# Retention in a two-layer mixer kernel: key decays applied to the values, query decays applied behind the states' products, states laid out by head parity

## The chip, the cores and the metric

One core of a Trainium2 chip runs the whole program. The metric is device time in microseconds of one execution. The core has five engines that run side by side, each through its own instructions in order: TensorE (PE; its weight loads, PEld, are shown apart), VectorE (DVE), ScalarE (ACT), GpSimd (POOL) and SyncE (SP), which issues the DMA transfers here.

## The reference, cut to what matters

Two layers, each with an input projection, four token mixers and an output projection over 2048 + 256 tokens. The change lies in one mixer, retention, with 4 heads of 64 in two directions d:

```
q_dec = exp((idx + 1) * log_gamma)        # per head and position in the chunk
k_dec = exp((c - 1 - idx) * log_gamma)
c_dec = exp(c * log_gamma)
s_new = s * c_dec + einsum('bhcd,bhce->bhde', k * k_dec, v)
o     = einsum('bhcd,bhde->bhce', q * q_dec, s) + einsum('bhij,bhje->bhie', att, v)
```

`k_dec` and `q_dec` are one number per token, head and direction. So k_dec may scale the rows of v in place of those of k, and q_dec may scale the rows of the product q s in place of those of q.

## The kernel before, in words

Tokens are worked in 18 tiles of 128 (`NT`), a retention chunk being one tile. Each layer has four passes. **A** normalises, projects and convolves. **B** holds the chunk-wise work: `gdn_tile` for another mixer, many 64x64 products, and `ret_tile` for retention, beside its projection (`dense`) and the state scans. **C** projects and runs sliding-window attention (`swa_tile`), finishes the scans, and forms the mixers' outputs (`ret_out`, `gdn_out`). **D** is the output projection.

In pass B `ret_tile` copies v (L753), rotates q and k, writes `kd`, the keys times both directions' decays (VectorE, L769), and multiplies: per head `kd` (128 tokens by 128 = direction and feature) by v gives the tile's addition to the state, `KV`, stored in DRAM with the directions in partitions 0 to 63 and 64 to 127. Then `qd`, the queries times both decays (GpSimd, L783), four transposes of q and k (L787), four of `qd` (L793), copies of both by ScalarE (L789, L795), and the store of the transposed `qd` as `Qr` (L796). The local attention follows. `ret_scan` carries the state over the tiles and stores it as `Sr`. In pass C `ret_out` loads `Qr`, `Sr` and the local part, makes one product per head, in which the sum over 128 partitions covers both directions, adds (L853), and normalises per head.

Matrix products go through the helper `mm`, so nearly all of them have line 145; their tiles tell them apart. An f32 product is two records in the trace, an f32 transpose one. A product with 128 rows and 128 columns of weights uses TensorE whole (`128*128` in a row); with 64 columns it uses one of two halves side by side (`128*64`), with 64 rows one of two halves above each other (`64*128`), with both one of four quarters (`64*64`). These are called modes below. PSUM banks are handed out by name: `pm` is a pair (`pm0`, `pm1`), each with one buffer, taken in turn by `self.pm()`.

The order of the instructions on each engine is fixed when the program is built: `weave` interleaves the passes' generators, and `Plan` then sorts all instructions by a table of costs and by the length of the work behind them. Any change of the work so draws the whole order anew.

Of the kernel before, what the change touches and what calls it, by code (L numbers as in the profile page):

```python
# [16 lines left out]
NT = 18  # L17
# [3 lines left out]
TC = 1  # L21
LU = 4
OWN = 1
PMAP = dict(x.split(":") for x in "ptk:0 ptv:h1 pt:0 pu:1 ptq:1 pm0:0 pm1:1 pc0:h0 pc1:h1 po:1 p3:1 rkv:h0 rpt:0 rpt2:0 rpo:h0 ch:h0".split())
PMAP.update(x.split(":") for x in ''.split())
CV = 4
NB = 9
# [6 lines left out]
MULT, ADD, SUB, MAXO, MINO = ALU.mult, ALU.add, ALU.subtract, ALU.max, ALU.min  # L34
# [33 lines left out]
           ("rqkT", 512, 2), ("ratt", 512, 1), ("rD", 512, 1), ("rlo", 256, 1)],  # L68
          [("gA00", 256, 1), ("gQ1", 512, 1), ("gR1", 1024, 1), ("gW1", 1024, 1), ("gMC1", 1024, 1)]),
    "C": ([("sqk", 384, 1), ("sks", 384, 1), ("srope", 256, 2), ("rota", 256, 1), ("rotb", 256, 1), ("sVc", 128, 2), ("sV", 128, 5),  # L70
           ("sqs", 512, 1), ("szt", 512, 1), ("szl", 512, 1), ("shs", 512, 1), ("roq", 512, 1), ("goq", 512, 1), ("goS", 512, 1),
           ("roS", 256, 1), ("roo", 256, 1), ("roz", 256, 1), ("rosq", 256, 1), ("goo", 256, 1), ("gosq", 256, 1), ("goz", 256, 1),
           ("roy", 256, 1), ("goy", 256, 1), ("sy", 256, 2), ("sPT", 640, 2), ("szb", 512, 2), ("sP", 640, 2)],
          [("sqT", 1024, 4)],
# [50 lines left out]
class Net:  # L125
# [134 lines left out]
    def setup(self):  # L260
        nc, cp, dp = self.nc, self.cp, self.dp
        C = self.t(cp, [128, C_W], "C")
        nc.sync.dma_start(C, self.consts[:, :C_W])
        self.C = C
        self.id = C[:, C_ID:C_ID + 128]
        self.bfid = self.t(cp, [128, 128], "bfid", BF)
        nc.vector.tensor_copy(self.bfid, self.id)
        self.bfm = self.t(cp, [128, 256], "bfm", BF)
        ml = self.t(Area([self.U], []), [128, 256], "cml")
        nc.sync.dma_start(ml, self.consts[:, T_ML:T_ML + 256])  # L270
        nc.vector.tensor_copy(self.bfm, ml)
# [12 lines left out]
        self.hT = self.t(dp, [NB, 128, 2 * KT * 256], "hTd")
        self.x1 = self.t(dp, [NTOK, D], "x1")
        self.modd = self.t(dp, [DEPTH, 2, 3 * D], "modd")
        self.gcd = self.t(dp, [NT, 8, 128], "gcd")
        self.hg = self.t(dp, [NB, 128, 6, 256], "hgd")
        self.gz = self.t(dp, [NT, 128, 256], "gzd")
        self.rz = self.t(dp, [NT, 128, 256], "rzd")  # L290
        self.MC = self.t(dp, [36, 128, 512], "MCd")
        self.Sg = self.t(dp, [36, 128, 256], "Sgd")
        self.Qg = self.t(dp, [NT, 128, 512], "Qgd")
        self.Qr = self.t(dp, [NT, 128, 512], "Qrd")
        self.KV = self.t(dp, [NT, 128, 256], "KVd")
        self.Sr = self.t(dp, [NT, 128, 256], "Srd")
        self.Og = self.t(dp, [NT, 128, 256], "Ogd")
        self.Or = self.t(dp, [NT, 128, 256], "Ord")
        self.law = self.t(dp, [NB, 128, 2, 2, 256], "lawd")
        self.hl = self.t(dp, [NB, 128, 2, 256], "hld")  # L300
        self.hb = self.t(dp, [NB, 128, 2, 256], "hbd")
        self.yT = self.t(dp, [NB, 128, 8, 256], "yTd")
# [405 lines left out]
    def ret_setup(self, sp):  # L708
        nc, C = self.nc, self.C
        sm = Area([self.ab.rearrange('p t u -> p (t u)')], [])  # L710
        lg = self.t(sm, [128, 8], "rlg")
        x = self.t(sm, [128, 8], "rlx")
# [13 lines left out]
        io = C[:, C_IOTA:C_IOTA + 4]  # L726
        self.qdec = self.t(sm, [128, 4, 2], "rqd")
        self.kdec = self.t(sm, [128, 4, 2], "rkd")
        self.cdec = self.t(self.lp, [128, 4], "rcd")
        for d in range(2):  # L730
            nc.vector.tensor_scalar(self.qdec[:, :, d], lg[:, 4 * d:4 * d + 4], io[:, 2 * d:2 * d + 1], None, op0=MULT)
            nc.vector.tensor_scalar(self.kdec[:, :, d], lg[:, 4 * d:4 * d + 4], io[:, 2 * d + 1:2 * d + 2], None, op0=MULT)
            nc.vector.tensor_scalar(self.cdec[64 * d:64 * d + 64], lg[64 * d:64 * d + 64, 4 * d:4 * d + 4], 128.0, None, op0=MULT)
        for a in (self.qdec, self.kdec, self.cdec):
            nc.scalar.activation(a, a, AF.Exp)

# [10 lines left out]
    def ret_tile(self, t, pa, pb, pp):  # L747

        nc = self.nc
        q_on = t >= 2 or not self.last  # L750
        qk = self.t(pp, [128, 512], "rqk", bufs=2)
        v = self.t(pp, [128, 256], "rv", bufs=2)
# [10 lines left out]
        else:  # L763
# [1 line left out]
            nc.sync.dma_start(rp, self.rope[(t - 2) * 128:(t - 1) * 128, 0:256])  # L765
            self.rotate(qk[:, :256], pa[:, :256], 4, rp[:, 0:64], rp[:, 64:128], pp)
            self.rotate(qk[:, 256:], pa[:, 256:], 4, rp[:, 128:192], rp[:, 192:256], pp)
        kd = self.t(pp, [128, 4, 2, 64], "rdd")
        nc.vector.tensor_tensor(kd, qk[:, 256:].rearrange("p (h e) -> p h e", h=4)[:, :, None].to_broadcast([128, 4, 2, 64]),  # L769
                                self.kdec[:, :, :, None].to_broadcast([128, 4, 2, 64]), op=MULT)  # L770
        self.taken += 1
        yield 0, 4.02
        pkv = self.slot("rkv", True)
        for h in range(4):
            self.mm(pkv[:, h * 64:(h + 1) * 64], kd[:, h].rearrange("p d e -> p (d e)"), v[:, h * 64:(h + 1) * 64])
        kv = self.t(pp, [128, 256], "rlo")
        nc.scalar.copy(kv, pkv[:, :256])
        self.st('K').dma_start(self.KV[t], kv)
        yield 0.86, 0
        if not q_on:  # L780
            return
        qd = self.t(pp, [128, 4, 2, 64], "rdd")
        nc.gpsimd.tensor_tensor(qd, qk[:, :256].rearrange("p (h e) -> p h e", h=4)[:, :, None].to_broadcast([128, 4, 2, 64]),  # L783
                                self.qdec[:, :, :, None].to_broadcast([128, 4, 2, 64]), op=MULT)
        pt = self.slot("rpt")
        for i in range(4):
            nc.tensor.transpose(pt[:, i * 128:(i + 1) * 128], qk[:, i * 128:(i + 1) * 128], self.id)  # L787
        qkT = self.t(pp, [128, 512], "rqkT", bufs=2)
        nc.scalar.copy(qkT, pt)  # L789
        yield 0.44, 0.84  # L790
        pt2 = self.slot("rpt2")
        for h in range(4):
            nc.tensor.transpose(pt2[:, h * 128:(h + 1) * 128], qd[:, h].rearrange("p d e -> p (d e)"), self.id)  # L793
        qdT = self.t(pp, [128, 512], "rqkT", bufs=2)
        nc.scalar.copy(qdT, pt2)  # L795
        self.st('Q').dma_start(self.Qr[t], qdT)  # L796
        yield 0.44, 2
        pat = self.sc2()
        for hp in range(2):
            for par in range(2):  # L800
# [5 lines left out]
        po = self.slot("rpo", True)  # L806
# [7 lines left out]
    def ret_scan(self, lo, hi):  # L814
        nc = self.nc
        if lo == 0:
            self.rS = self.t(self.lp, [128, 4, 64], "rS", bufs=2)
            nc.vector.memset(self.rS, 0.0)
        fl = lambda a: a.rearrange("p h e -> p (h e)")
        for i in range(lo, hi):  # L820
            S = self.rS
            tf, tb = i, ORDER_B[i]
            yield lambda: tf in self.kvs and tb in self.kvs
            self.st('S').dma_start(self.Sr[tf, 0:64], fl(S)[0:64])
            self.st('S').dma_start(self.Sr[tb, 64:128], fl(S)[64:128])
            self.rstep = i
            if i == NT - 1:
                break
            kv = self.t(self.lp, [128, 4, 64], "rsk", bufs=2)
            nc.sync.dma_start(fl(kv)[0:64], self.KV[tf, 0:64])  # L830
            nc.sync.dma_start(fl(kv)[64:128], self.KV[tb, 64:128])
            S2 = self.t(self.lp, [128, 4, 64], "rS", bufs=2)
            nc.vector.tensor_tensor(S2, S, self.cdec[:, :, None].to_broadcast([128, 4, 64]), op=MULT)
            nc.vector.tensor_tensor(S2, S2, kv, op=ADD)
            self.rS = S2
            yield 0, 1.5

    def ret_out(self, t, pp):

        nc = self.nc  # L840
        s = t % 2
        q = self.t(pp, [128, 512], "roq")
        nc.sync.dma_start(q, self.Qr[t])
        S = self.t(pp, [128, 256], "roS")
        nc.sync.dma_start(S, self.Sr[t])
        o0 = self.t(pp, [128, 256], "roo")
        nc.sync.dma_start(o0, self.Or[t])
        zz = self.t(pp, [128, 256], "roz")
        nc.sync.dma_start(zz, self.rz[t])
        po = self.pm()  # L850
        for h in range(4):
            self.mm(po[:, h * 64:(h + 1) * 64], q[:, h * 128:(h + 1) * 128], S[:, h * 64:(h + 1) * 64])
        nc.vector.tensor_tensor(o0, po[:, :256], o0, op=ADD)  # L853
        o4 = o0.rearrange("p (h e) -> p h e", h=4)
        mu = self.t(pp, [128, 4], "romu")
        nc.vector.tensor_reduce(mu, o4, axis=AX.X, op=ADD)
        nc.vector.tensor_scalar(mu, mu, 1.0 / 64, None, op0=MULT)
# [9 lines left out]
        pt = self.pm()  # L867
# [1173 lines left out]
```

## Time and profile before

| | |
|---|---|
| median of 3 runs | 3140.94 us (3136.82 to 3141.93) |
| the profiled execution | 3140.24 us, its span 3138.5 us |
| PE busy | 2940.4 us, 94% of the span |
| VectorE, ScalarE, GpSimd busy | 62%, 43%, 39% |
| mean granted TensorE clock | 0.969 |

The span runs from the first to the last instruction, and 1.7 us lie around it. PE counts as busy while any matmul is in flight, so 94% says where the time goes, not how well TensorE is filled.

### The profile page before, as it was taken

To read this page: it belongs to the slowest core of one execution; us is meant where nothing else is said; L and a number is where in the kernel's file an instruction comes from. 1 tells how busy PE (TensorE), PEld (TensorE's weight loads), DVE (VectorE), ACT (ScalarE), POOL (GpSimd) and SP (SyncE) were. 2 spreads that over 40 slices of the span, in tenths; PEclk is the share of its full clock that TensorE was granted. 3 is DMA by queue.
4 is the path that set the end of the run, shared out by engine and by line. 5 is a ranking of instruction groups with operands and counts; after the bars stand their busy time and mean duration, and the time that the engine had idled before them with its cause. 6 is when DMAs were issued, how large, how long until landed. Compare 5 with 4: busy or idle time off the path is not lost. (4 is left out here: it accounts for less than half of the span.)

```text
span 3138.5 us, 78206 instructions
## 1 busy us (share of the span) xinstructions
PE 2940.4 (94%) x31820; PEld 2497.3 (80%) x31820; DVE 1938.9 (62%) x4258; ACT 1334.3 (43%) x2930; POOL 1220.2 (39%) x1197
## 2 busy tenths in 40 slices
PE   4999979999999999979999998899999899999987
PEld 3999867778877888867789998678878688888766
DVE  4587777676665576653255787767666456767321
ACT  3466644444443344442134666444444424445211
POOL 2133345555542232334352333456555422323332
PEclk8999989999999999999999999999999999999998
DMA  7243465554456655375652435556444664544431
GB/s 275 95 173 134 166 168 150 167 153 118 134 180 187 199 163 162 122 264 196 197 202 106 162 144 162 161 150 176 141 140 120 220 198 139 171 152 142 153 122 68
DMA packets 410121, 504.69 MB, mean 161 GB/s; under 512 B 94056, under 2 KB 311560, under 8 KB 403104
## 3 DMA queue, kind: packets, MB, share of 16 engines
q1 hardware_dynamic: 409760, 499.68, 49.7%
q8 instruction: 250, 4.10, 0.5%
q14 instruction: 111, 0.91, 0.1%
HBM read 320.06 MB, written 179.50 MB: 159 GB/s over the span
## 5 line engine op out<-in xcount | busy, mean ns | idle before, releaser
L145 PE MATMUL pd<-w,h 128*128 128x512 f32 (+1 forms) x3408 | 984.4, 411 | 26.2 <-DVE U L1560 16.1
L145 PEld LDWEIGHTS pd<-w,h 128*128 128x128 f32 x3408 | 613.4, 192 | 158.6 <-ACT U L1558 18.5
L145 PE MATMUL pd<-h,w 128*128 128x256 f32 x3360 | 589.2, 294 | 1.1 <-DVE U L479 1.1
L145 PEld LDWEIGHTS pd<-h,w 128*128 128x128 f32 x3360 | 479.8, 193 | 10.6 <-issue 5.0
L330 POOL TENSOR_TENSOR U<-U,mh 128x4 f32<-128x4 f32 (+2 forms) x174 | 179.5, 1034 | 379.6 <-DVE U L329 361.2
L145 PE MATMUL pg<-h,w 128*128 128x256 f32 x1680 | 294.3, 294 | 4.7 <-DVE U L1571 3.6
L145 PE MATMUL pm<-U 128*64 128x128 f32 (+4 forms) x3280 | 249.4, 274 | 26.4 <-ACT U L1089 7.7
L145 PEld LDWEIGHTS pg<-h,w 128*128 128x128 f32 x1680 | 245.0, 191 | 9.9 <-DVE U L1571 3.8
L145 PEld LDWEIGHTS pm<-U 128*64 128x64 f32 (+2 forms) x3280 | 197.6, 143 | 68.4 <-issue 22.3
L145 PE MATMUL pg<-w,h 128*128 128x512 f32 x816 | 228.6, 394 | 1.3 <-DVE U L1571 1.3
L145 PEld LDWEIGHTS <-U 64*64 64x64 f16 x6512 | 153.2, 109 | 55.1 <-issue 45.4
L145 PE MATMUL pg<-U 64*64 64x64 f16 x6512 | 188.4, 195 | 1.2 <-DVE U L1031 1.1
L145 PEld LDWEIGHTS pg<-w,h 128*128 128x128 f32 x816 | 154.4, 190 | 38.8 <-issue 3.3
L1031 DVE TENSOR_TENSOR U<-pg,C 128x512 f16<-128x512 f32 x180 | 122.0, 684 | 64.3 <-PE pg L145 63.5
L625 DVE SCALAR_TENSOR_TENSOR U<-U 128x256 f32<-128x256 f32 x318 | 159.8, 552 | 1.1 <-POOL U L558 1.1
L1560 DVE TENSOR_TENSOR U<-U 128x1 f32<-128x1 f32 x34 | 7.7, 230 | 234.9 <-ACT U L1558 234.9
L1456 ACT ACTIVATE U<-sc,U 128x640 f32<-128x640 f32 (+2 forms) x136 | 104.2, 766 | 103.7 <-DVE U L1454 88.5
L1471 ACT COPY U<-pg 128x512 f32<-128x512 f32 (+2 forms) x248 | 100.7, 436 | 103.6 <-PE pg L1470 50.1
L1558 ACT ACTIVATE U<-pd 128x512 f32<-128x512 f32 x34 | 20.0, 594 | 276.7 <-PE pd L145 164.4
L1453 DVE TENSOR_REDUCE U<-sc 128x1 f32<-128x640 f32 (+2 forms) x136 | 106.2, 781 | 47.3 <-PE sc L145 45.7
L1046 DVE STREAM_TRANSPOSE U<-U 128x512 f16<-128x512 f16 x144 | 100.8, 703 | 45.8 <-ACT U L1042 45.3
L1042 ACT CAST U<-pg 128x512 f16<-128x512 f32 x144 | 84.0, 588 | 82.9 <-PE pg L145 77.9
(297 smaller groups left out, 6038.3 us busy)
## 6 DMA issues: line engine op xcount, KB each, us to landing
hTd<-h SPq DMA_DIRECT2D x18, 2048.0 KB, 6.7
h<-hTd SPq DMA_DIRECT2D x72, 512.0 KB, 5.6
h<-hTd SPq DMA_DIRECT2D x18, 2048.0 KB, 9.8
MCd<-U SPq DMA_DIRECT2D x72, 256.0 KB, 3.3
cMC<-MCd SPq DMA_DIRECT2D x140, 128.0 KB, 3.3
U<-yTd SPq DMA_DIRECT2D x34, 512.0 KB, 4.5
U<-in_w_in_dram SPq DMA_DIRECT2D x58, 256.0 KB, 3.9
hgd<-U SPq DMA_DIRECT2D x53, 256.0 KB, 2.5
```

Source lines behind the costliest of these rows:

```text
L145: self.nc.tensor.matmul(out, lhsT, rhs, start=start, stop=stop)
L330: nc.gpsimd.tensor_tensor(out, out, self.mh[:, :n], op=ALU.pow)
L625: nc.vector.scalar_tensor_tensor(z[:, i], xb[:, f, j:j + 256], cw[:, f, j:j + 1], z[:, i], op0=MULT, op1=ADD)
L1031: nc.vector.tensor_tensor(M, p1, lev(k), op=MULT)
L1042: nc.scalar.copy(Y, p2)
L1046: nc.vector.transpose(fl(YT), fl(Y))
L1453: nc.vector.tensor_reduce(m[:, h:h + 1], pv, axis=AX.X, op=MAXO)
L1456: nc.scalar.activation(p[:, :nk], pv, AF.Exp, bias=m[:, h:h + 1], accum_out=sums[:, h:h + 1])
L1471: nc.scalar.copy(pT[:, a:a + w], pt[:, :w])
L1558: nc.scalar.activation(x1[:, 512 * k:512 * k + 512], po[k], AF.Square, accum_out=ss[:, k:k + 1])
L1560: nc.vector.tensor_tensor(rs, ss[:, 0:1], ss[:, 1:2], op=ADD)
```

## The change

`kd` is gone: `vd`, the values times both directions' decays, takes its place (same engine, same shape), and the product per head is now k (64 columns of weights) by `vd` (128 columns), so heads of even number fill partitions 0 to 63 and those of odd number 64 to 127. `qd`, its four transposes and their copy are gone; the transposed q, unscaled, is stored instead, half as wide. State, scan and their DRAM tensors are laid out to match: direction outside, parity of the head in the partitions; their transfers are as many as before. In `ret_out` each head's product takes 64 rows, and gives the two directions beside each other (128 columns); the heads of one parity go to one `pm` bank, those of the other to the second. Eight operations of VectorE then each scale 64 columns by the query's decay and add them, where one addition of 256 columns stood.

```diff
-        kd = self.t(pp, [128, 4, 2, 64], "rdd")
-        nc.vector.tensor_tensor(kd, qk[:, 256:].rearrange("p (h e) -> p h e", h=4)[:, :, None].to_broadcast([128, 4, 2, 64]),
+        vd = self.t(pp, [128, 4, 2, 64], "rdd")
+        nc.vector.tensor_tensor(vd, v.rearrange("p (h e) -> p h e", h=4)[:, :, None].to_broadcast([128, 4, 2, 64]),
                                 self.kdec[:, :, :, None].to_broadcast([128, 4, 2, 64]), op=MULT)
...
+        pk4 = pkv[:, :256].rearrange("p (d a f) -> p d a f", d=2, a=2)
         for h in range(4):
-            self.mm(pkv[:, h * 64:(h + 1) * 64], kd[:, h].rearrange("p d e -> p (d e)"), v[:, h * 64:(h + 1) * 64])
+            self.mm(pk4[64 * (h % 2):64 * (h % 2) + 64, :, h // 2], qk[:, 256 + h * 64:256 + (h + 1) * 64], vd[:, h])
...
-        qd = self.t(pp, [128, 4, 2, 64], "rdd")
-        nc.gpsimd.tensor_tensor(qd, qk[:, :256].rearrange("p (h e) -> p h e", h=4)[:, :, None].to_broadcast([128, 4, 2, 64]),
-                                self.qdec[:, :, :, None].to_broadcast([128, 4, 2, 64]), op=MULT)
...
-        pt2 = self.slot("rpt2")
-        for h in range(4):
-            nc.tensor.transpose(pt2[:, h * 128:(h + 1) * 128], qd[:, h].rearrange("p d e -> p (d e)"), self.id)
-        qdT = self.t(pp, [128, 512], "rqkT", bufs=2)
-        nc.scalar.copy(qdT, pt2)
-        self.st('Q').dma_start(self.Qr[t], qdT)
-        yield 0.44, 2
+        self.st('Q').dma_start(self.Qr[t], qkT[:, :256])
...
-        po = self.pm()
-        for h in range(4):
-            self.mm(po[:, h * 64:(h + 1) * 64], q[:, h * 128:(h + 1) * 128], S[:, h * 64:(h + 1) * 64])
-        nc.vector.tensor_tensor(o0, po[:, :256], o0, op=ADD)
+        po = [self.pm()[:, :256].rearrange("p (a d f) -> p a d f", a=2, d=2) for _ in range(2)]
+        for a in range(2):
+            for par in range(2):
+                r = slice(64 * par, 64 * par + 64)
+                self.mm(po[par][:, a], q[r, a * 128:(a + 1) * 128], S[r, :, a])
         o4 = o0.rearrange("p (h e) -> p h e", h=4)
+        for d in range(2):
+            for h in range(4):
+                nc.vector.scalar_tensor_tensor(o4[:, h], po[h % 2][:, h // 2, d], self.qdec[:, h, d:d + 1], o4[:, h], op0=MULT, op1=ADD)
```

The order on PE at the first retention tile of pass B in layer 0, before; `sc_3904` holds the KV products, L787 transposes q and k, L793 `qd`, `pd` is dense work:

```order
L145 MATMUL sc_3904<-G_233 128x64 x4
L787 MATMUL pm_184_4079<-C_96,G_233 128x128 x4
L980 MATMUL pm_185_4085<-C_96,U_87 128x128 x4
L145 MATMUL pd_4178<-w_2_88,h_171_3905 128x512 x2
L793 MATMUL pm_186_4097<-C_96,G_233 128x128 x4
L145 MATMUL sc_3904<-U_87 64x64 x16
```

The same place after the change (lines moved up by one to three; the second `sc_3904` row is the local attention):

```order
L145 MATMUL sc_3904<-G_233 64x2x64 x4
L786 MATMUL pm_184_4078<-C_96,G_233 128x128 x4
L977 MATMUL pm_185_4084<-C_96,U_87 128x128 x4
L145 MATMUL sc_3904<-G_233 128x128 x4
L145 MATMUL pd_4171<-w_2_88,h_171_3905 128x512 x3
```

The KV products are still four in a row, now 64 partitions by 2 x 64, and the transposes of L793 have no row any more.

The order on PE at the third `ret_out` of pass C in layer 0, before; `pm_755` holds its products, `pd` is dense work, `pg` and `sc` belong to the attention:

```order
L1470 MATMUL pg_772_14404<-C_96,U_87 128x128 x2
L145 MATMUL pd_14547<-h_741_14156,w_2_88 128x256 x3
L145 MATMUL pm_755_14270<-U_87 128x64 x4
L1407 MATMUL pm_764_14348<-C_96,U_87 128x128 x2
L145 MATMUL pd_14547<-h_741_14156,w_3_89 128x256 x3
```

And after, where `pm_740` and `pm_739` hold the two parities, and eleven other rows lie between their two groups:

```order
L145 MATMUL pd_14453<-h_725_14046,w_6_92 128x256 x2
L145 MATMUL pd_14453<-h_725_14046,w_7_93 128x256 x3
L145 MATMUL pm_740_14161<-U_87 128x128 x2
L145 MATMUL pd_14453<-h_725_14046,w_8_94 128x256
L145 MATMUL sc_14220<-G_13504,F_13503 128x256 x2
```

The second piece, from the same stretch:

```order
L1467 MATMUL pg_751_14259<-C_96,U_87 128x128 x2
L145 MATMUL sc_14270<-G_13504,F_13503 128x256 x2
L145 MATMUL pd_14453<-h_725_14046,w_3_89 128x256 x2
L145 MATMUL pm_739_14160<-U_87 128x128 x2
L145 MATMUL pd_14453<-h_725_14046,w_3_89 128x256
```

What stood as one group of four is now two groups of two, each of one parity, with whole-array work between. Over the 34 `ret_out` of both layers the 64-row products stand in 56 groups, of which 3 alternate the two halves. Counted over all of PE's order, the mode changes between neighbours 1271 times before and 1380 times after: in the stretches of pass B 893 and 900 times, in those from the end of pass B on (passes C, D, and A of the second layer) 368 and 468 times, ahead of the first pass B 8 and 10 times, and twice at the seams.

The order on VectorE at the same `ret_out`, before (L853 is the addition, L1454 and L1398 the attention's):

```order
L1454 TENSOR_SCALAR U_87<-U_87,rb_236 128x1
L853 TENSOR_TENSOR U_87<-pm_755_14270,U_87 128x256
L856 TENSOR_REDUCE U_87<-U_87 128x4
L857 TENSOR_SCALAR U_87<-U_87 128x4
L1398 TENSOR_TENSOR U_87<-U_87 128x2x64
```

And after:

```order
L1451 TENSOR_SCALAR U_87<-U_87,rb_236 128x1
L851 SCALAR_TENSOR_TENSOR U_87<-pm_739_14160,ab_252,U_87 128x64 x4
L851 SCALAR_TENSOR_TENSOR U_87<-pm_740_14161,ab_252,U_87 128x64 x4
L1342 SCALAR_TENSOR_TENSOR U_87<-U_87 128x512
L853 TENSOR_REDUCE U_87<-U_87 128x4
```

Eight operations on the two banks stand where one on a single bank stood (`ab` holds the decays).

## Rows read from the trace of the kernel before

Times are in microseconds from the span's start unless marked otherwise; "x136" is a count, "mean ns" that of one instruction. In the groups by form the columns behind the count are busy us, mean ns of one, and the idle us before them with what ended it.

**Rows 1.** The page: the span, and part 1's row of the engines
```profile
span 3138.5 us, 78206 instructions
PE 2940.4 (94%) x31820; PEld 2497.3 (80%) x31820; DVE 1938.9 (62%) x4258; ACT 1334.3 (43%) x2930; POOL 1220.2 (39%) x1197
```

**Rows 2.** Busy time by stretch: steady passes B and C of both layers
```profile
core 0: us, PE busy (x) PEld busy (x) DVE busy (x) ACT busy (x) POOL busy (x), PEclk, DMA share, GB/s
430.00:960.00 530.00, 521.15 (x9006) 415.37 (x9006) 347.33 (x654) 223.67 (x458) 278.70 (x246) 1.00 0.53 154
1040.00:1360.00 320.00, 314.04 (x2706) 278.52 (x2704) 227.36 (x637) 153.44 (x418) 98.23 (x121) 0.99 0.49 156
2010.00:2460.00 450.00, 449.37 (x8097) 359.03 (x8098) 300.59 (x583) 194.78 (x396) 247.78 (x219) 1.00 0.51 147
2580.00:2880.00 300.00, 291.20 (x2514) 257.92 (x2512) 206.08 (x574) 140.46 (x385) 87.74 (x110) 0.98 0.47 147
```

**Rows 3.** Groups by form, TensorE's matmuls (PE) and weight loads (PEld), line 793
```profile
L793 PE MATMUL pm<-C,G 128*128 128x128 f32 x136 | 22.1, 284 | 0.0
L793 PEld LDWEIGHTS pm<-C,G 128*128 128x128 f32 x136 | 15.8, 142 | 4.0 <-issue 1.7
```

**Rows 4.** Groups by form, weight loads of small f32 matmuls on line 145
```profile
L145 PEld LDWEIGHTS pm<-U 128*64 128x64 f32 x1824 | 94.3, 141 | 35.1 <-issue 9.0 <-ACT U L1471 8.1 <-DVE U L853 5.0
L145 PEld LDWEIGHTS sc<-G 128*128 128x128 f32 x560 | 73.3, 195 | 16.9 <-DVE G L769 10.6 <-DVE F L999 1.6 <-DVE G L804 0.5
L145 PEld LDWEIGHTS pm<-U 128*128 128x128 f32 x304 | 39.5, 193 | 7.4 <-ACT U L1242 5.4 <-DVE U L1230 0.8
L145 PEld LDWEIGHTS sc<-G 64*128 64x128 f32 x272 | 18.5, 186 | 8.2 <-issue 5.7 <-ACT G L795 0.4 <-ACT U L1106 0.4
```

**Rows 5.** Timeline, PE: a tile's KV products (pass B), a ret_out's (pass C)
```profile
509.84 1.00 PE L145 MATMUL sc<-G 128*128 128x64 f32 x8
510.67 0.60 PE L1105 MATMUL pm<-C,U 128*128 128x128 f32 x4
...
1116.75 1.00 PE L145 MATMUL pm<-U 128*128 128x64 f32 x8
1117.58 0.28 PE L1470 MATMUL pg<-C,U 128*128 128x128 f32 x1
```

**Rows 6.** Timeline, PE, pass C: transposes ahead of a mode change, and without
```profile
1109.15 0.38 PE L869 MATMUL pm<-C,U 128*128 128x128 f32 x2
1109.46 0.43 PE L145 MATMUL pm<-U 128*64 128x128 f32 x2
1109.82 0.98 PE L145 MATMUL pd<-h,w 128*128 128x256 f32 x6
...
1113.16 0.38 PE L1199 MATMUL pm<-C,U 128*128 128x128 f32 x2
1113.30 0.95 PE L145 MATMUL pd<-h,w 128*128 128x256 f32 x6
```

**Rows 7.** Timeline, PEld, the same place: idle time ahead of the loads
```profile
1109.46 0.19 PEld L145 LDWEIGHTS pm<-U 128*64 128x64 f32 x2 [0.17 <-issue]
1109.82 0.54 PEld L145 LDWEIGHTS pd<-h,w 128*128 128x128 f32 x4 [0.17 <-issue]
```

**Rows 8.** Groups by form, VectorE: readings of PSUM, and the shortest operation
```profile
L1479 DVE TENSOR_TENSOR U<-pm,U 128x128 f32<-128x128 f32 x68 | 19.4, 286 | 28.1 <-PE pm L145 27.2
L853 DVE TENSOR_TENSOR U<-pm,U 128x256 f32<-128x256 f32 x34 | 14.3, 419 | 18.6 <-DMA U<-Ord 9.3 <-PE pm L145 9.3
L1458 DVE TENSOR_TENSOR U<-U 128x1 f32<-128x1 f32 x136 | 29.3, 215 | 49.7 <-ACT U L1457 43.8 <-ACT U L1456 5.4
```

**Rows 9.** Groups by form, GpSimd and ScalarE: the two operations taken out
```profile
L783 POOL TENSOR_TENSOR G<-G,ab 128x512 f32<-128x512 f32 x34 | 37.9, 1113 | 73.9 <-PE sc L145 72.6 <-DVE U L954 1.0
...
L795 ACT COPY G<-pm 128x512 f32<-128x512 f32 x34 | 20.0, 587 | 34.9 <-PE pm L793 32.5 <-DMA KVd<-G 2.3
```

**Rows 10.** Timeline, PE, end of pass C, layer 0: its longest wait
```profile
1390.80 2.46 PE L145 MATMUL pm<-U 128*64 128x128 f32 x16 [6.51 <-ACT U L1471]
```

More of the change, by code (lines that the diff above doesn't have):

```diff
@@ L23 @@
 OWN = 1
-PMAP = dict(x.split(":") for x in "ptk:0 ptv:h1 pt:0 pu:1 ptq:1 pm0:0 pm1:1 pc0:h0 pc1:h1 po:1 p3:1 rkv:h0 rpt:0 rpt2:0 rpo:h0 ch:h0".split())
+PMAP = dict(x.split(":") for x in "ptk:0 ptv:h1 pt:0 pu:1 ptq:1 pm0:0 pm1:1 pc0:h0 pc1:h1 po:1 p3:1 rkv:h0 rpt:0 rpo:h0 ch:h0".split())
 PMAP.update(x.split(":") for x in ''.split())
@@ L70 @@
     "C": ([("sqk", 384, 1), ("sks", 384, 1), ("srope", 256, 2), ("rota", 256, 1), ("rotb", 256, 1), ("sVc", 128, 2), ("sV", 128, 5),
-           ("sqs", 512, 1), ("szt", 512, 1), ("szl", 512, 1), ("shs", 512, 1), ("roq", 512, 1), ("goq", 512, 1), ("goS", 512, 1),
+           ("sqs", 512, 1), ("szt", 512, 1), ("szl", 512, 1), ("shs", 512, 1), ("roq", 256, 1), ("goq", 512, 1), ("goS", 512, 1),
            ("roS", 256, 1), ("roo", 256, 1), ("roz", 256, 1), ("rosq", 256, 1), ("goo", 256, 1), ("gosq", 256, 1), ("goz", 256, 1),
@@ L293, in setup @@
         self.Qg = self.t(dp, [NT, 128, 512], "Qgd")
-        self.Qr = self.t(dp, [NT, 128, 512], "Qrd")
-        self.KV = self.t(dp, [NT, 128, 256], "KVd")
-        self.Sr = self.t(dp, [NT, 128, 256], "Srd")
+        self.Qr = self.t(dp, [NT, 128, 256], "Qrd")
+        self.KV = self.t(dp, [NT, 2, 128, 128], "KVd")
+        self.Sr = self.t(dp, [NT, 2, 128, 128], "Srd")
         self.Og = self.t(dp, [NT, 128, 256], "Ogd")
@@ L728, in ret_setup @@
         self.kdec = self.t(sm, [128, 4, 2], "rkd")
-        self.cdec = self.t(self.lp, [128, 4], "rcd")
+        self.cdec = self.t(self.lp, [128, 2, 2], "rcd")
         for d in range(2):
@@ L732, in ret_setup @@
             nc.vector.tensor_scalar(self.kdec[:, :, d], lg[:, 4 * d:4 * d + 4], io[:, 2 * d + 1:2 * d + 2], None, op0=MULT)
-            nc.vector.tensor_scalar(self.cdec[64 * d:64 * d + 64], lg[64 * d:64 * d + 64, 4 * d:4 * d + 4], 128.0, None, op0=MULT)
+            r = slice(64 * d, 64 * d + 64)
+            nc.vector.tensor_scalar(self.cdec[r], lg[r].rearrange("p (d a b) -> p d a b", d=2, a=2)[:, :, :, d], 128.0, None, op0=MULT)
         for a in (self.qdec, self.kdec, self.cdec):
@@ L773, in ret_tile @@
         pkv = self.slot("rkv", True)
+        pk4 = pkv[:, :256].rearrange("p (d a f) -> p d a f", d=2, a=2)
         for h in range(4):
-            self.mm(pkv[:, h * 64:(h + 1) * 64], kd[:, h].rearrange("p d e -> p (d e)"), v[:, h * 64:(h + 1) * 64])
+            self.mm(pk4[64 * (h % 2):64 * (h % 2) + 64, :, h // 2], qk[:, 256 + h * 64:256 + (h + 1) * 64], vd[:, h])
         kv = self.t(pp, [128, 256], "rlo")
         nc.scalar.copy(kv, pkv[:, :256])
-        self.st('K').dma_start(self.KV[t], kv)
+        self.st('K').dma_start(self.KV[t].rearrange("d p n -> p d n"), kv.rearrange("p (d n) -> p d n", d=2))
         yield 0.86, 0
@@ L816, in ret_scan @@
         if lo == 0:
-            self.rS = self.t(self.lp, [128, 4, 64], "rS", bufs=2)
+            self.rS = self.t(self.lp, [128, 2, 2, 64], "rS", bufs=2)
             nc.vector.memset(self.rS, 0.0)
-        fl = lambda a: a.rearrange("p h e -> p (h e)")
+        fl = lambda a: a.rearrange("p a e -> p (a e)")
         for i in range(lo, hi):
@@ L823, in ret_scan @@
             yield lambda: tf in self.kvs and tb in self.kvs
-            self.st('S').dma_start(self.Sr[tf, 0:64], fl(S)[0:64])
-            self.st('S').dma_start(self.Sr[tb, 64:128], fl(S)[64:128])
+            self.st('S').dma_start(self.Sr[tf, 0], fl(S[:, 0]))
+            self.st('S').dma_start(self.Sr[tb, 1], fl(S[:, 1]))
             self.rstep = i
@@ L828, in ret_scan @@
                 break
[L829 to L833, printed above, removed]
+            kv = self.t(self.lp, [128, 2, 2, 64], "rsk", bufs=2)
+            nc.sync.dma_start(fl(kv[:, 0]), self.KV[tf, 0])
+            nc.sync.dma_start(fl(kv[:, 1]), self.KV[tb, 1])
+            S2 = self.t(self.lp, [128, 2, 2, 64], "rS", bufs=2)
+            nc.vector.tensor_tensor(S2, S, self.cdec[:, :, :, None].to_broadcast([128, 2, 2, 64]), op=MULT)
             nc.vector.tensor_tensor(S2, S2, kv, op=ADD)
@@ L841, in ret_out @@
         s = t % 2
-        q = self.t(pp, [128, 512], "roq")
+        q = self.t(pp, [128, 256], "roq")
         nc.sync.dma_start(q, self.Qr[t])
-        S = self.t(pp, [128, 256], "roS")
-        nc.sync.dma_start(S, self.Sr[t])
+        S = self.t(pp, [128, 2, 2, 64], "roS")
+        nc.sync.dma_start(S.rearrange("p d a f -> p d (a f)"), self.Sr[t].rearrange("d p n -> p d n"))
         o0 = self.t(pp, [128, 256], "roo")
```

## The prediction

> **What bounds the kernel now.** I read the page first. PE is busy for 94% of the span, no other engine for more than 62% [rows 1]. Since "busy" is a mean over passes, I then cut the span into its steady stretches, two of pass B and two of pass C [rows 2]: PE is in flight for 521 of 530 us and 449 of 450 in B, for 314 of 320 and 291 of 300 in C, while VectorE has 66% and 67% in B, 71% and 69% in C. PE waits long only at the passes' ends, as where one product waits 6.5 us for the attention's copy [rows 10]. So in the stretches where retention works the end moves by what TensorE's stream gains or loses, and other engines' work is covered as long as PE finds other work ahead of it. PEclk is 0.98 to 1.00 there, so no gain is to be had from the clock. The sum is made against the profiled execution, 3140.24 us; the median of the runs is 0.7 us above it. A measurement of this kernel can tell about 0.2%, some 6.3 us, from no change; the line to "faster" is so at 3134.7.
>
> **The transposes taken out.** 136 transposes on L793 go, four for each of 34 tiles. Their weight loads are busy for 15.8 us, 116 ns each, and their matmuls for 22.1, in which part of a neighbour's flight is counted [rows 3]. I take the loads: **-15.8 us**, bounds -12 and -22 (12: some overlap with a neighbour in any case).
>
> **The KV products.** 36 tiles with four products, eight records, each. Now such a group holds PE for 0.83 us from its start to the next start [rows 5]; the loads of this form take 73.3 / 560 = 131 ns a record when all its groups are counted [rows 4]. After the change the weights have 64 columns and the moving operand 128. The nearest row is that of the attention's and the other mixer's output, 94.3 / 1824 = 52 ns a record [rows 4], in which neighbours alternate between the two halves, as the four heads do here. Eight make 0.41 us, 0.42 less: **-15.1 us** for 36. Bounds: -5 (the pace of 64*128, 18.5 / 272 = 68 ns, and no alternation) and -17.
>
> **The products of ret_out.** 34 tiles, eight records each, 0.83 us [rows 5]. With 64 rows and alternating halves a record is 68 ns [rows 4], which would save 0.29 us a tile. But in the order only 3 of the 56 groups alternate; the others load the same half again and again, for which the nearest row is a whole-array load of 39.5 / 304 = 130 ns [rows 4], about what it costs now. I take 3 of 34 tiles: **-0.9 us**; bounds -9.9 and 0. The Trainium skill ("TensorEngine Tiling (Array Packing)", "Theoretical Speedup") gives up to twofold for a contract dimension of at most 64. By it these products would save 14.1 us; no run here shows it for groups that stay on one half.
>
> **The mode changes.** The order has 109 more of them, 100 outside pass B's stretches, nearly all at the two-part groups of ret_out. What one costs is read at a place of pass C [rows 6]: two transposes hold PE for 0.31 us ahead of one, for 0.14 where none follows, so 0.17 going in; two records of `128*64` hold it for 0.36 us, of which their own pace explains 0.10, so 0.26 coming out. PEld stands idle for 0.17 us at each [rows 7]. I take 0.2 us: **+21.8 us**, bounds +5 (a change costs nothing beside a wait, or where it falls among changes that stood already) and +28 (0.26 each). The Trainium skill's same page ("Key Properties") says that a change of mode drains TensorE; by that rule, the idle 0.17 us agrees.
>
> **VectorE in ret_out.** One addition of 256 columns out of PSUM takes 419 ns, one of 128 columns 286 ns [rows 8]; the line through both gives 220 ns at 64 columns, between the 215 ns of the shortest operation and 286. Eight make 1.76 us, 1.34 more than now; 34 tiles: 45.6 us more of VectorE, all in pass C, whose share goes from 71% and 69% to some 78%. PE's dense and attention work covers it in the middle; at the two ends of pass C nothing does, and there the last tile's chain is 1.34 us longer: **+2.7 us**; bounds 0 and +45.6 (no cover at all). The Trainium skill ("VectorE: DVE Perf Modes", "The TRN2 errata") speaks against many small operations, since each pays a fixed latency. Its 120 + 64 cycles at 0.96 GHz would make 1.53 us of the eight, and 37.9 us of the 45.6.
>
> **What costs nothing.** GpSimd loses 34 operations of 1.1 us and ScalarE 34 copies of 0.59 us [rows 9]: both lie beside a PE that is 98 to 100% busy in pass B, and both engines have room there. `vd` takes the engine and shape of `kd`, and depends on v alone, so the KV products wait for the rotation of k instead of for one VectorE operation behind it; a start that comes earlier gives PE nothing while it is not idle. The transfers are as many as before on SP's queue; the stored q is half as large, the rows of `KV` and `Sr` come in pieces half as long, and DMA is busy for 0.47 to 0.53 in these stretches [rows 2]. If that cover were gone, the first sign would be ret_out's products waiting for their loads. Two `pm` banks are now taken together, held for some 2.6 us (0.83 and 1.76); a rival below is made of that.
>
> **The sum.** -15.8 - 15.1 - 0.9 + 21.8 + 2.7 = -7.3 us: 3140.2 - 7.3 = **3133 us**. Pass B gains some 29 us (two terms less nine changes at 0.2), passes C lose some 22.
>
> **Rivals.**
> 1. *The mode changes cost little, or the halves overlap after all*: a change beside products of other modes is paid already. With the lower bounds, -15.8 - 15.1 - 0.9 + 5 = -27, so 3113 us, and 3104 if ret_out's products also reach 68 ns. For it: PE's stream around ret_out is full of attention transposes and 64x64 products. Against: the place read is of just this kind.
> 2. *The pair of banks becomes the bound of pass C*: the next user of `pm0` or `pm1` in PE's fixed order stands behind eight additions in place of one, and everything on PE behind it waits too. At half of the 45.6 us this gives -7.3 - 2.7 + 22.8 = +13, 3153 us; in full 3176. It decides from the point where that next user stands less than 1.8 us of PE's work behind the products. Against: the loads of this form waited 5.0 us for L853 in all so far [rows 4], and the order puts ten and more rows behind them.
> 3. *The gain of pass B is smaller and the changes dearer*: KV products at half their gain (-7.5) and 0.26 us a change (+28.3): -15.8 - 7.5 - 0.9 + 28.3 + 2.7 = +6.8, 3147 us.
>
> **How the numbers follow.** I give the forecast 0.45, rival 1 0.25, rival 2 0.15, rival 3 0.15. The forecast's own range, 3126 to 3140, is cut by the line at 3134.7: 0.25 of it faster, 0.20 same. With rival 1: faster 0.50. Rival 3 lies just over the line on the other side, 0.03 of it within; so same 0.23, slower 0.27. The range reaches from rival 1 with all its bounds, 3104, to half of rival 2 with some room, 3157; outside it I leave rival 2 in full and an order drawn anew that is worse or better than all of this.
>
> **What would show it.** Right: in pass B's stretches the same work ends some 14 us earlier in each layer, at the same PE share; KV products' loads near 52 ns; PEld idle ahead of ret_out's groups near 0.2 us; eight operations of about 220 ns. Wrong: loads of ret_out's products near 68 ns, or groups that follow a change with no gap (rival 1); PE waiting in pass C for L851, with idle of a microsecond and more (rival 2); KV products near 0.7 us a tile (rival 3).

## The result and the profile after

The change made the kernel a little slower: 3157.97 us in the first four runs (3148.86 to 3160.95), a ratio of 1.0053 to before, 95% interval 1.0035 to 1.0071; on another chip, with twelve runs, 3155.04 us and 1.0033 (1.0020 to 1.0045). The forecast was 3133; its range ended at 3157, just under the first median and just over the second. The profiled execution took 3160.66 us.

The head of the page after, which answers to [rows 1]:

```profile
span 3158.9 us, 78104 instructions
PE 2945.3 (93%) x31684; PEld 2478.7 (78%) x31684; DVE 1987.7 (63%) x4496; ACT 1317.8 (42%) x2896; POOL 1194.6 (38%) x1163
```

TensorE lost 136 instructions and is in flight 5 us longer. Where the time went is seen when both spans are cut at the ends of the passes (A, B, C, D of layer 0, then of layer 1). Columns as in [rows 2]. Before:

```profile
0.00:405.10 405.10, 353.96 (x2626) 327.36 (x2626) 275.75 (x588) 218.71 (x411) 116.08 (x146) 0.96 0.46 166
405.10:946.30 541.20, 521.04 (x8953) 415.16 (x8953) 363.28 (x685) 229.61 (x472) 291.38 (x255) 0.98 0.54 155
946.30:1393.60 447.30, 422.83 (x3715) 367.27 (x3715) 294.26 (x828) 194.84 (x533) 132.07 (x159) 0.97 0.55 173
1393.60:1624.30 230.70, 221.59 (x996) 166.49 (x992) 71.97 (x113) 52.61 (x113) 90.98 (x62) 0.98 0.61 212
1624.30:1957.90 333.60, 320.98 (x2472) 311.55 (x2473) 246.09 (x512) 190.23 (x359) 108.92 (x131) 0.98 0.41 148
1957.90:2494.10 536.20, 515.82 (x8848) 414.16 (x8847) 359.50 (x710) 234.96 (x484) 286.91 (x252) 0.98 0.53 154
2494.10:2940.00 445.90, 418.37 (x3546) 363.02 (x3544) 284.32 (x752) 184.59 (x494) 127.14 (x150) 0.96 0.52 164
2940.00:3138.50 198.50, 165.79 (x672) 132.28 (x672) 43.73 (x77) 28.70 (x70) 66.73 (x44) 0.92 0.32 110
```

After:

```profile
0.00:405.90 405.90, 354.60 (x2626) 327.41 (x2626) 274.86 (x587) 218.84 (x411) 116.02 (x145) 0.96 0.46 166
405.90:932.60 526.70, 504.24 (x8867) 399.22 (x8868) 357.74 (x686) 219.60 (x453) 271.07 (x237) 0.97 0.53 153
932.60:1410.20 477.60, 440.18 (x3727) 377.09 (x3725) 323.21 (x954) 196.26 (x534) 135.37 (x160) 0.96 0.51 158
1410.20:1640.00 229.80, 222.92 (x996) 166.15 (x996) 71.26 (x112) 52.80 (x113) 91.46 (x62) 0.98 0.62 214
1640.00:1978.50 338.50, 324.19 (x2479) 313.69 (x2480) 249.71 (x524) 193.33 (x366) 112.48 (x132) 0.96 0.40 146
1978.50:2507.90 529.40, 508.57 (x8766) 401.80 (x8766) 362.47 (x700) 222.44 (x460) 271.98 (x236) 0.96 0.54 155
2507.90:2958.40 450.50, 424.13 (x3557) 361.26 (x3555) 304.72 (x863) 185.89 (x494) 129.55 (x150) 0.97 0.49 154
2958.40:3158.90 200.50, 166.46 (x672) 132.12 (x672) 43.70 (x76) 28.66 (x70) 66.69 (x44) 0.91 0.31 108
```

Pass B gained 14.5 us in layer 0 and 6.8 in layer 1. Pass C lost 30.3 and 4.6. In the first pass C TensorE's busy time rose by 17 us and its idle time from 24.5 to 37.4. The granted clock is 0.01 to 0.02 lower in both passes B, in the first C and in A of layer 1. Over all runs the lower clock is more than the whole of the loss. For each execution I split the span in two: span times granted clock (what the span would be with the clock always full, waits included), and the rest, called **lost to the clock** here.

| | span x clock | lost to the clock |
|---|---|---|
| before (29 runs) | 3045.7 | 94.8 |
| after (12 runs, same chip) | 3037.3 | 114.3 |

So at full clock the change gains 8.4 us, and the clock takes 19.5 back. (That 8.4 lies near the forecast's 7.3 is luck: errors in several of its terms cancel, as told below.) A stretch at the lower clock lies at the end of nearly every wait of TensorE of 2 us and more, or starts within 3 us behind it: at 29 of 31 in the traced execution of after, at 23 of 28 in that of before. One of after, in 4-us windows (columns as above):

```profile
1304.00:1308.00 4.00, 3.92 (x44) 3.21 (x43) 3.16 (x14) 2.71 (x9) 1.10 (x2) 1.00 0.44 113
1308.00:1312.00 4.00, 4.00 (x35) 3.90 (x36) 3.93 (x12) 1.44 (x4) 1.23 (x2) 1.00 0.95 365
1312.00:1316.00 4.00, 1.08 (x10) 0.87 (x8) 0.27 (x2) 0.00 (x0) 1.01 (x1) 0.90 0.96 345
1316.00:1320.00 4.00, 2.81 (x13) 2.84 (x14) 1.63 (x5) 1.66 (x4) 1.49 (x2) 0.50 0.24 80
1320.00:1324.00 4.00, 4.00 (x27) 3.40 (x27) 3.00 (x7) 0.91 (x3) 1.64 (x2) 0.75 0.07 24
```

From 1315.2 us on, for 6.8 us, the clock is at 0.50, the lower level (1.2 GHz). It falls during the wait of 4.12 us in this row of the timeline of PE (start, duration, and in brackets the idle time ahead):

```profile
1317.19 1.08 PE L1412 MATMUL pm<-C,U 128*128 128x128 f32 x4 [4.12 <-DVE U L1451]
```

L1412 are the attention's transposes into a `pm` bank. VectorE stood at gdn_out's addition, which reads such a bank:

```profile
1316.62 0.42 DVE L1181 TENSOR_TENSOR U<-pm,U 128x256 f32<-128x256 f32 x1 [4.35 <-DMA U<-Ogd]
```

So a late load delays VectorE, which delays TensorE, which then runs at half clock for some microseconds more (here until 1322.0 us). The Trainium skill ("TensorE: Matmul & The Clock Gate", "HAM oscillation — how this bites in real kernels") tells of such waits for data, behind which the next work starts at the lower clock; the windows above agree.

The changed operations themselves, by form (as [rows 4] and [rows 8]):

```profile
L145 PEld LDWEIGHTS pm<-U 64*128 64x128 f32 x272 | 30.6, 193 | 11.2 <-issue 4.8 <-ACT F L1417 1.5 <-DVE rS L826 0.4
L145 PEld LDWEIGHTS sc<-G 128*64 128x64 f32 x288 | 16.0, 141 | 16.0 <-DVE G L770 8.3 <-issue 2.7 <-DVE F L996 2.0
```

```profile
L851 DVE SCALAR_TENSOR_TENSOR U<-pm,ab,U 128x64 f32<-128x64 f32 x272 | 57.9, 276 | 22.5 <-PE pm L145 17.6 <-DMA U<-Ord 4.7
```

A record of the KV products loads for 16.0 / 288 = 56 ns, one of ret_out's for 30.6 / 272 = 112 ns. The eight operations are busy for 57.9 / 272 = 213 ns each (forecast 220).

### The profile page after: what moved, and what is told of

The parts are those of the page before. It is cut to its first block, busy times and chain, and to the rows that moved or that the text cites. A ratio compares the mean times of both kernels' runs of the same rounds, so it can differ in the third digit from the quotient of the medians.

```text
span 3158.9 us, 78104 instructions
## 1 busy us (share of the span) xinstructions
PE 2945.3 (93%) x31684; PEld 2478.7 (78%) x31684; DVE 1987.7 (63%) x4496; ACT 1317.8 (42%) x2896; POOL 1194.6 (38%) x1163
## 5 line engine op out<-in xcount | busy, mean ns | idle before, releaser
L145 PEld LDWEIGHTS pd<-h,w 128*128 128x128 f32 x3360 | 484.0, 194 | 14.5 <-issue 5.1
L145 PEld LDWEIGHTS pm<-U 128*64 128x64 f32 (+3 forms) x3280 | 195.2, 143 | 57.9 <-issue 22.4
L145 PEld LDWEIGHTS <-U 64*64 64x64 f16 x6624 | 166.8, 110 | 61.4 <-issue 52.0
L145 PE MATMUL pg<-U 64*64 64x64 f16 x6624 | 205.2, 196 | 2.7 <-DVE U L1028 2.6
L145 PE MATMUL sc<-G,F 128*128 128x256 f32 (+1 forms) x528 | 111.2, 324 | 12.0 <-ACT U L1453 10.4
```

What stands on the lines that cost most here:

```text
L145: self.nc.tensor.matmul(out, lhsT, rhs, start=start, stop=stop)
```

## Experiments

"Held" means that the planner still sees the operations of the unedited kernel, so that every engine issues the same work at the same place. The columns are the median, its ratio to the kernel before in the same rounds with its 95% interval, and means over all runs. "After, again" is the unchanged kernel after in the rounds of the second chip; "one bank" and "two banks" are kernels of experiments 2 and 4.

| kernel | median us | ratio | lost to the clock | span x clock |
|---|---|---|---|---|
| after, again | 3155.0 | 1.0033 (1.0020 to 1.0045) | 114.3 | 3037.3 |
| before, TURN 27 | 3140.3 | 0.9997 (0.9986 to 1.0009) | 97.3 | 3040.3 |
| before, lateness 560 | 3143.4 | 1.0004 (0.9994 to 1.0013) | 96.6 | 3045.2 |
| after, TURN 27 | 3147.4 | 1.0017 (1.0007 to 1.0027) | 105.6 | 3037.4 |
| after, lateness 560 | 3174.1 | 1.0101 (1.0088 to 1.0114) | 124.5 | 3048.0 |
| after, held, 128 rows | 3140.6 | 1.0004 (0.9995 to 1.0012) | 109.3 | 3030.8 |
| after, held, h later | 3148.3 | 1.0020 (1.0008 to 1.0031) | 110.3 | 3034.6 |
| after, held, two of eight | 3150.3 | 1.0027 (1.0016 to 1.0038) | 113.9 | 3035.3 |
| before, held, eight | 3149.7 | 1.0028 (1.0017 to 1.0039) | 97.4 | 3052.0 |
| before, held, 64 rows | 3153.3 | 1.0035 (1.0023 to 1.0048) | 97.7 | 3054.2 |
| one bank | 3121.8 | 0.9939 (0.9917 to 0.9961) | 96.2 | 3024.6 |
| one bank, TURN 27 | 3131.0 | 0.9957 (0.9944 to 0.9970) | 101.4 | 3027.6 |
| one bank, lateness 560 | 3125.6 | 0.9940 (0.9928 to 0.9953) | 103.0 | 3019.0 |
| two banks | 3142.8 | 1.0004 (0.9993 to 1.0016) | 110.7 | 3029.5 |
| two banks, TURN 27 | 3141.1 | 0.9996 (0.9984 to 1.0007) | 105.2 | 3034.7 |
| two banks, lateness 560 | 3147.1 | 1.0012 (1.0000 to 1.0024) | 114.6 | 3030.1 |

**1. Is it only the luck of the order?** The first theory (W) was that the redrawn order had put waits at bad places; the rival (S) that the new products and additions lengthen pass C in any order. First other orders of both kernels:

```diff
-TURN = 25.0
+TURN = 27.0
```

> The kernel before, with the planner's constant TURN at 27 instead of 25: the same instructions, drawn in another order. Theory W (waits of the redrawn order, each followed by a stretch at the low clock, gave the gain back): order alone moves this kernel by 5 to 25 us, more likely up than down, and what is left of the span after TensorE's idle time and half of its time at the low clock stays within 5 us of the 2843.7 of before. Theory S (the change itself lengthens pass C, by mode changes and the eight additions): an order drawn anew is worth little, the time stays within 6 us of before.

> The kernel after with TURN at 27 instead of 25: the same instructions as after, drawn in another order. Theory W: the time can be anywhere from 3115 to 3165 us, as idle time and low clock fall out, and the rest of the span (without idle time and half of the low clock) is within 5 us of the 2824.0 of after. Theory S: 3152 to 3165 us, since the mode changes and the additions are as many.

Then, the order held, the mode changes taken out of after, and its large loads moved:

```diff
-                self.mm(po[par][:, a], q[r, a * 128:(a + 1) * 128], S[r, :, a])
+                self.mm(po[par][:, a], q[:, a * 128:(a + 1) * 128], S[:, :, a])
```

> The kernel after, every engine's order held as it is; the four products of a ret_out group read all 128 rows of the queries and of the states instead of 64, so that each holds the sum over both heads of a pair (this part of the computation is changed). What is gone are the mode changes around the groups, some 100 in passes C. Theory S: 100 x 0.2 us, so 15 to 22 us faster than after. Theory W: the changes cost 0.1 us or less each, 0 to 10 us faster than after, and the waits of 2 to 5 us in the first layer's pass C are still there.

```diff
+        for k in [k for k in sp if tag(self.ins[k].ins) == "hTd" and self.prod(d[1] for d in self.ins[k].outs[0].bass_ap.ap) == 1 << 19]:
+            p = sp.index(k)
+            late = [q for q in range(p + 1, p + 5) if tag(self.ins[sp[q]].ins) in ("Ogd", "MCd")]
+            if late:
+                sp.insert(late[-1], sp.pop(p))
```

> The kernel after, the order of TensorE, VectorE, ScalarE and GpSimd held; on SyncE ten of the 2-MB loads of h in passes C stand one to four places later, behind the small loads of gdn_out's sums and of the scan's matrices. Theory W: the waits of TensorE at 1216, 1317 and 2841 us for VectorE's chain (3.1, 4.1 and 3.1 us) and the one at 1052 us for the matrices (5.3 us) shrink to under 1 us each and the low clock behind them goes, 10 to 25 us faster than after. Theory S: no difference beyond 3 us, or slower where h itself comes late.

Another order moved before by nothing measurable, against W. The order of after moves it more, to 3147 us, inside W's wide range and under the 3152 that S had as its least; but both stay above before. W's second test came out: TensorE's busy time less half of its time at the low clock moved by 1 us in before and by 2 in after. Without mode changes after is 0.0029 faster, 9 us: half of S's price, at the upper end of W's. (Against the first four runs of after, 1.0053, it would be 15 us.) With the loads moved, VectorE's waits for gdn_out's load fell from 18.3 us to 6.3, and the wait at 1317 us went; that at 1216 us stayed (3.65), others of 3.1 and 4.3 us came. 4 us faster, inside the intervals: W's own experiment did not bear it out.

**2. VectorE's eight operations, and whole-array products.** Theory V: the longer VectorE chain makes TensorE wait. Six of the eight were taken out of after, and eight put into before (four with the products, four with zero times the products), orders held:

```diff
+                if 0 < 4 * d + h < 7:
+                    self.dropped.add(self.nc.cur_bb.bb.instructions[-1].name)
...
+            seq = [k for k in seq if self.ins[k].name not in gone]
```

> The kernel after, unchanged, for a comparison on the same chip with the three below. Every theory: 3148 to 3161 us, the granted clock about 0.963 against 0.970 of before, and the span times the clock some 7 us under that of before.

> The kernel after, every engine's order held; of the eight operations of VectorE that add ret_out's products, six are left out (one of each bank stays; this part of the computation is left out), so that VectorE has as little to do there as before the change. Theory V (the longer VectorE work delays the chains of gdn_out and attention that TensorE waits for in passes C, and the clock falls behind the waits): TensorE's idle time in the two passes C falls from 64 to some 50 us, the granted clock rises to 0.967 or more, 10 to 20 us faster than after. Theory W (waits come from loads that the redrawn order put at bad places): the waits at 1216, 1317 and 2841 us stay, under 5 us faster.

```diff
-        nc.vector.tensor_tensor(o0, po[:, :256], o0, op=ADD)
+        for d in range(2):
+            for h in range(4):
+                nc.vector.scalar_tensor_tensor(o4[:, h], po[:, h * 64:h * 64 + 64], 1.0 - d, o4[:, h], op0=MULT, op1=ADD)
```

> The kernel before, every engine's order held; the one addition of 256 columns in ret_out is replaced by eight operations of VectorE of 64 columns with the form of those of after (four add the products, four add zero times the products), so that only VectorE's part of the change is made. Theory V: 10 to 20 us slower than before, with new waits of TensorE of 1 to 4 us in passes C and a granted clock of 0.967 or less. The forecast's cover (all hidden but the two ends): 0 to 3 us slower. Theory W: 0 to 3 us, since no load moves.

V falls in after: 2 us, not to be told from nothing, and the clock as low. In before the eight cost 0.0028, 9 us, 6 of them at full clock: not hidden, as the forecast's cover had it, and under V's 10. The fourth kernel keeps the change but for ret_out's products:

```diff
+        for par in range(2):
+            r = slice(64 * par, 64 * par + 64)
+            nc.sync.dma_start(S[r, par].rearrange("p d a f -> p d (a f)"), self.Sr[t, :, r].rearrange("d p n -> p d n"))
-        po = [self.pm()[:, :256].rearrange("p (a d f) -> p a d f", a=2, d=2) for _ in range(2)]
+        po = self.pm().rearrange("p (a c d f) -> p a c d f", a=2, c=2, d=2)
         for a in range(2):
+            self.mm(po[:, a], q[:, a * 128:(a + 1) * 128], S[:, :, :, a])
```

> The kernel after, but ret_out's states are stored into a tile with zeros, one block for each head of a pair, so that two products of 128 rows and 256 columns replace four of 64 rows and 128 columns, into one bank instead of two; the planner draws the order anew. The computation is complete. The mode changes around the groups are gone. Theory S: the span without idle time and half of the low clock falls from 2824 to some 2813 us, as where the order was held. What idle time and clock make of it is open by theory W: 3122 to 3152 us; by theory V it keeps a clock of 0.963 to 0.966, 3140 to 3150 us, since the eight operations stay.

It takes 3121.8 us, 20 less than before and 33 less than after, with the clock of before. That is at the edge of what W left open, and V, by which the eight additions keep the clock low, is out. S missed too: TensorE's busy time less half of its time at the low clock is some 3 us under that of after, not 11.

**3. Does it hold in other orders?** Theory M: the form of ret_out's products brings the low clock, whatever the order. A third order of each kernel, and a second of the one with one bank:

```diff
-LATE = 600, 150, 1200
+LATE = 560, 150, 1200
```

> The kernel after, with the planner's constant for lateness on TensorE at 560 instead of 600: the same instructions in a third order (after 600 and TURN 25; the first redrawn one had TURN 27). The time lost to the low clock (span times one minus the granted clock, mean over runs) was 114 us in the first order and 106 in the second. Theory W (luck of the order): it can be anywhere from 94 to 117 us, and the time from 3128 to 3160 us. Theory M (the two-bank products of 64 rows themselves bring the low clock): 104 us or more, 3142 us or more.

> The kernel before with the same constant at 560: a third order of its instructions. It lost 94 us in its own order and 97 with TURN 27. Theory W: anywhere from 92 to 117 us, 3135 to 3162 us. Theory M: 100 us or less, 3133 to 3148 us.

> The kernel with whole-array products in ret_out (two of 128 rows and 256 columns against states padded with zeros, one bank), with TURN at 27. In its first order it lost 96 us to the low clock and took 3121.8 us. Theory W: 94 to 117 us lost, 3118 to 3143 us. Theory M: 100 us or less, under 3128 us.

> The same kernel with whole-array products, with the constant for lateness at 560, its third order. Theory W: 94 to 117 us lost, 3118 to 3143 us. Theory M: 100 us or less, under 3128 us. By both it stays under the kernel after in the same order, by the 7 us at full clock that the mode changes cost where the order was held.

It holds. The medians in three orders are 3140 to 3143 us for before, 3147 to 3174 for after and 3122 to 3131 for the one-bank kernel, and the three do not overlap. W's ranges ended below the third order of after (124.5 us lost, 3174). Two of the one-bank kernels lost a little more to the clock (101, 103) than M's line of 100, and one took 3131 instead of under 3128.

**4. The pair of banks or the mode changes?** Theory B says the first, theory C the second.

```diff
-        po = self.pm().rearrange("p (a c d f) -> p a c d f", a=2, c=2, d=2)
+        po = [self.pm()[:, :256].rearrange("p (c d f) -> p c d f", c=2, d=2) for _ in range(2)]
```

> The kernel with whole-array products in ret_out, but its two products go to two banks taken together, as in after, instead of one; no mode changes around them, eight additions, order drawn anew. Theory B (the pair of banks makes the order bad): the loss to the low clock is that of after, 105 us or more, and the time 3138 to 3160 us. Theory C (the mode changes do it): as with one bank, 103 us or less, 3118 to 3133 us.

> The same with two banks, second order (TURN 27; after took 3147 us in it, the one with one bank 3131). Theory B: 3140 us or more. Theory C: 3135 us or less.

> The same with two banks, third order (lateness 560; after took 3174 us in it, the one with one bank 3126). Theory B: 3150 us or more. Theory C: 3133 us or less.

```diff
-            self.mm(po[:, h * 64:(h + 1) * 64], q[:, h * 128:(h + 1) * 128], S[:, h * 64:(h + 1) * 64])
+            r = slice(64 * (t % 2), 64 * (t % 2) + 64)
+            self.mm(po[:, h * 64:(h + 1) * 64], q[r, h * 128:(h + 1) * 128], S[r, h * 64:(h + 1) * 64])
```

> The kernel before, every engine's order held; ret_out's four products of a tile read 64 of the 128 rows of queries and states (one direction of the scan alone, so that part of the computation is left out), which puts mode changes around its groups and changes nothing else. Theory C: the span at full clock rises by some 7 us, as it fell where they were taken from after, and the loss to the low clock by 5 to 20 us more: 3150 to 3168 us. Theory B: the 7 us alone, 3144 to 3150 us.

Both cost time. The second bank, with the order that is drawn for it, costs 0.0065, 0.0039 and 0.0072 in the three pairs, 18 us in the mean: 8 at full clock (3023.7 to 3031.4), 10 lost to the clock (100.2 to 110.2). So B's figures hold, but for the third (3150 or more), missed at 3147. C missed all three; it holds in its own term only: the mode changes alone cost before 0.0035, 11 us, of which 8 at full clock and 3 lost to the clock, where C had 5 to 20 and B none.

Where the second bank may bite is seen in the list of TensorE's waits (us in total, times, longest). L1416 is here the row that is L1412 in after, L1185 gdn_out's addition. One bank:

```profile
PE pm L1416 <- DVE U L1185: 10.9, 7, 2.9
PE pm L1416 <- DVE cS L1169: 2.6, 1, 2.6
PE pm L1416 <- DVE U L1459: 1.4, 1, 1.4
```

Two banks:

```profile
PE pm L1416 <- DVE U L1185: 19.4, 8, 3.5
PE pm L1416 <- DVE U L1455: 2.6, 1, 2.6
```

Together 14.9 against 22.0 us. In the order with TURN 27, one bank and then two:

```profile
PE pm L1416 <- DVE U L1185: 7.7, 5, 2.6
PE pm L1416 <- DVE U L1459: 6.9, 3, 3.8
```

```profile
PE pm L1416 <- DVE U L1185: 21.6, 9, 3.4
```

In the order with lateness 560:

```profile
PE pm L1416 <- DVE U L1185: 12.7, 8, 3.4
```

```profile
PE pm L1416 <- DVE U L1185: 15.3, 7, 3.3
PE pm L1416 <- DVE U L1459: 3.4, 1, 3.4
PE pm L1416 <- DVE U L1455: 2.9, 1, 2.9
```

That is 14.6 against 21.6 and 12.7 against 21.6. `pm` has two banks, and ret_out, gdn_out and the attention's transposes share them. When ret_out takes both at a time, these transposes wait longer in all, mostly for gdn_out's addition, which reads such a bank. How far this makes the 18 us is not shown. Another row of the attention's transposes (L1408) went the other way in the order with TURN 27, from 12.5 to 3.5 us. All waits of TensorE together were 185.1, 210.4 and 195.6 us with one bank, and 193.7, 207.0 and 200.9 with two. And in after itself the row, there L1412, waits 13.1, 20.1 and 11.8 us in the three orders, hardly more than with one bank. So the price of the second bank is measured with whole-array products and orders drawn anew; in after it was not measured by itself. The Trainium skill ("TensorEngine Tiling (Array Packing)", "Gotcha 1: PSUM Pressure") says that products on different rows of the array go to different banks and so press on PSUM; here a second bank, in products of all 128 rows, cost 18 us.

## Why the forecast was wrong

**What bounds the kernel** was read rightly as TensorE's stream. Two steps built on that reading failed. From the full clock in the stretches of [rows 2] the forecast took it that the clock has no part in the sum; over the whole span the clock cost 19.5 us. And it held that in the middle of pass C TensorE always finds other work to cover VectorE's. In after, the first stretch of pass C reads

```profile
1040.00:1360.00 320.00, 298.81 (x2420) 261.04 (x2420) 223.66 (x667) 138.09 (x376) 87.02 (x108) 0.96 0.42 133
```

where TensorE was in flight for 314.04 us at a clock of 0.99 before: new waits of 5.3, 3.6, 3.1, 2.0 and 4.1 us lie in the middle of the pass. Such a wait costs twice, its own time and the low clock behind it. Even before the change the long waits were not only at the passes' ends, as the forecast read them: four of 2.0 to 3.5 us lie in the two stretches of pass C. And only some 9 of the 95 us that before loses to the clock fall into the four stretches that it looked at.

**The transposes** are right: from start of group to start of the next, less idle time, the transposes of retention and gates (`pm<-C,G`) hold TensorE 59.0 us before and 43.0 after, -16.0 against -15.8 forecast.

**The KV products** gain less. Measured the same way their groups fall from 33.1 us (the form `sc<-G 128*128 128x64` in both traces, 65.5 less 32.4) to 23.3, so -9.8 and not -15.1. The loads came near the forecast (56 ns), but a tile holds TensorE for 23.3 / 36 = 0.65 us and not 0.41: the pace of the loads is not the time that a group takes. Rival 3 had this part.

**The products of ret_out** were put at -0.9 us. Their groups held TensorE for 28.7 us before and 37.9 after, the gaps at the mode changes included; over all 128 rows, in the order of after, they held it for 30.9. So without the mode changes the products came out at +2.2.

**The mode changes** were priced at 21.8 us. Where the order is held they cost 9 us in after (1.0033 less 1.0004; each ratio is known to some 4 us) and 11 in before, gaps and low clock together. The first is for 96 changes fewer on TensorE, the second for 73 more, so 0.09 and 0.15 us each: the 0.2 us read at one place was too much, and in after about double.

**The additions** were put at +2.7 us; the held orders give 2 in after and 9 in before.

**The pair of banks** was costed at nothing, and that is the term that measured largest: 18 us, in the kernels with whole-array products. Rival 2 named the resource, but looked only at the eight additions that hold both banks. Its sign, waits of a microsecond and more for L851, did appear in after, though small: two waits of 4.7 us in all stand against 4.3 us for L853 before.

```profile
PE pm L1196 <- DVE U L851: 4.7, 2, 3.6
PE pm L145 <- DVE U L851: 0.3, 1, 0.3
```

With six of the eight additions left out, 3.1 us of these waits stayed, as many as in a second traced execution of after, so the number of additions is not what makes them.

With these terms the sum is -16.0 - 9.8 + 2.2 + 10 + 18 + 2 = +6 us, or +13 with the dearer price of the additions; measured were +10 (second chip) and +17. Each price is uncertain by some 4 us, and that of the banks comes from a neighbouring kernel, so the agreement proves little by itself. It is borne out in part by the one-bank kernel, which has neither the second bank nor the mode changes: without these two the sum is -22 to -15 us, and it came out 19, 14 and 19 us under before by its ratios. That the change gains at full clock about what the forecast said in all is luck: there the mode changes cost 6.5 us (3037.3 less 3030.8) and not 21.8, and against that stand 5.3 us less from the KV products and 8 us for the second bank.

Pass B did gain: 14.5 us in layer 0, as forecast, but 6.8 in layer 1, together 21.3 against some 29. Passes C lost 34.9, more than the forecast 22. What lifts the third order of after to 3174 us, 27 above two whole-array banks in the same order, stays open in the main. The mode changes explain some 10 of it, and there rival 2's sign is plain, 12.1 us against 1.5 with whole-array products:

```profile
PE pm L1196 <- DVE U L851: 7.0, 3, 3.6
PE pm L145 <- DVE U L851: 5.1, 2, 4.8
```

## What to carry to other kernels

Count the PSUM banks that an operation takes at a time, not only how long it holds them: here, with two banks and three users, taking both cost time in all three orders tried. When a change moves products to half the array, try first to fill the other half with zeros: here two products of 128 rows with zeros needed one bank and no mode change around them, and turned a loss of 0.3% into a gain of 0.6%. And on a kernel that keeps TensorE in flight for 94% of its span, price each new wait with the low clock behind it; span times granted clock against the rest shows in one line which of the two moved.

## What the chip showed beyond that

Where ret_out's four products read 128 rows instead of 64, their groups held TensorE for 30.9 us instead of 37.9 in the same order: half the rows was the slower form, gaps at the mode changes included. And repeated executions of one kernel in one order are up to 21 us apart (after with the loads moved: 3135.3 to 3156.6 in twelve; before with TURN 27: 3129.7 to 3147.9). The granted clock goes with it in part, as 0.967 and 0.965 in the first two, 0.971 and 0.966 in the others.
